# A fp32 encoder block on one core: the second norm's scale by way of HBM, a plain opening of the late up-projection units, and another order of the last steps

## The chip, the cores and the metric

The kernel runs on one core of one Trainium2 chip. A core has five engines with queues of their own, each working its queue strictly in the order in which it was written: TensorE (PE, matrix products, whose weight loads the profile shows as PEld), VectorE (DVE), ScalarE (ACT), GpSimd (POOL) and SyncE (SP). Transfers between HBM and the on-chip memory are issued from SP, ACT or POOL and run on 16 DMA engines. The metric is the device time of one execution in microseconds (us); the kernel before took 945.14 us, the median of three runs (944.67 to 945.18).

## The reference

One layer on x of 256 tokens by 2048 features, everything in float32:

```python
h = _rmsnorm(x, norm1_g)
proj = h @ w_in                                   # q | k | v | u
a = _rmsnorm(_window_attention(q, k, v, sink), attn_out_g)
f = _rmsnorm(_fourier_mix(u, w_fourier), fourier_out_g)
x = x + jnp.concatenate([a, f], axis=-1) @ w_out
x = x + _conv_ffn(_rmsnorm(x, norm2_g), w_up, dw_w, dw_b, w_down)
return _rmsnorm(x, normf_g)

def _conv_ffn(h, w_up, dw_w, dw_b, w_down):
    up = h @ w_up
    gate, val = up[..., :D_FF], up[..., D_FF:]     # D_FF = 5504 = 43 * 128
    gate = conv over the tokens, width 3, per channel (gate, dw_w) + dw_b
    act = jax.nn.gelu(gate, approximate=False) * val
    return act @ w_down
```

The change touches the second norm (its 1/sqrt of the mean square, one number for each token) and the feed-forward part.

## The kernel before, in words

**Two parts for each number.** A float32 product is made of three products of a faster type: each operand is split into a high part (ACT copies it, L180) and a low part (DVE subtracts, L181), and TensorE adds high by high, low by high and high by low into one PSUM bank. A *unit* is one 128x2048 block of weights (1 MB): SP loads it into one of three `raw` buffers (`load`, L160), `split` (L173) makes its parts in one of three `hi` and one of three `lo` buffers and issues the load of the unit three further on, and TensorE then works on it.

**Up-projection units.** For the 43 tiles of 128 channels there are a gate unit and a value unit each. Here the weights stand still and the tokens move (`still_weights`, L322): 16 products of a high weight tile with the high and low parts of the tokens (512 columns) and 16 of a low weight tile with their high parts (256 columns). The order is by default high, low, high, low. With `first = (1, 0)` one high product is taken ahead: high, high, low, high, ..., high, low, low.

**The second norm.** `hT2` holds the tokens turned so that features lie on partitions, scaled by the norm's weight. The other factor, 1/sqrt of the mean square of each token (`rstd_of(tot2, ...)`, a small DVE sum, a DVE multiply and a power on POOL, L279), is multiplied in behind the up-projection: `scaled_sum` (L843) adds the two halves of a unit's bank and multiplies by `r2b`, which has the 256 factors along its columns, the same on all 128 partitions. `spread` (L288) makes `r2b`: DVE builds two diagonal matrices, TensorE multiplies a matrix of ones with them (fp32, L296), DVE copies the bank to `r2b` (L299). The first norm does the same by way of HBM, on POOL's queue (`row_by_hbm`, L303): one transfer writes the 256 numbers as a row, a second reads that row into all partitions.

**Where that stands.** The last unit of the output projection still needs its sums when the feed-forward part begins, so the first two up units, gate0 and val0, are taken as a pair (L1137): twelve of sixteen steps of gate0, then the turning of the last quarter of the tokens (`turn_x(3)`), twelve steps of val0, the last four of both, and then `spread`.

**The feed-forward order.** `ff_items` (L84) writes out one list of items, which TensorE works through: up units ("u"), products of the down-projection ("s": 14 for each of five groups of channel tiles, in a two-level Strassen form with seven products P1, P7, N5, N3, P6, P2, N4 for each of two column halves c, 12 matmuls of 512 columns each, L1070 to L1072) and, in the last group, four "d" items (`("down", c)`, 24 matmuls) for the channel tiles 36 to 39. At the end four `last` units do the tiles 40 to 42 (L1214). `PATTERNS` (L72) gives the order within a group. N5, P6 and N4 use a sum of weight blocks in `sumw`, which POOL's adding transfers build in place: N5's split starts one (L966), P6's the next (L968).

**What an item does to the other queues.** `ff_step(n)` (L992) is called behind item n on TensorE. It first puts the posts of earlier items (`beside`), then the split of item n + 2, then further posts (`behind`). An up unit's posts are `scaled_sum` one item later, then the convolution (`gate_conv`), GELU and, for a value unit, `val_mult` and `act_parts`. A product's bank is added to the output by `product_out` one item later; P1 and N5 stay in their banks and are added by `shared_out` in three steps, the first behind the item that follows P6 of half 1. `down` items 0 and 1 add into the banks of P2 and N4 of the same half (`joined`), items 2 and 3 into banks of their own; `down_out` adds them to the output.

The changed line of the pattern stands for this order from item 141 on, where a number behind a name is the tile and (c=1) the column half:

| item | before | after |
|---|---|---|
| 143 to 149 | N4(c=0), down 0, val 40, P1, N5, gate 41, P7 | the same |
| 150 to 154 | val 41, N3, gate 42, P6, val 42 | N3, val 41, P6, gate 42, val 42 |
| 155 to 159 | P2, down 2, N4, down 1, down 3 | P2, N4, down 1, down 2, down 3 |

In the kernel before, all up units behind the first `down` (val 40, gate 41, val 41, gate 42, val 42) open with `first = (1, 0)`.

Of the kernel before, what the change touches and what calls it, by code (L numbers as in the profile page):

```python
# [8 lines left out]
F32 = mybir.dt.float32  # L9
F32R = mybir.dt.float32r  # L10
AF = mybir.ActivationFunctionType
ALU = mybir.AluOpType

P = 128
D = 2048
S = 256
NK = D // P
# [52 lines left out]


PATTERNS = ["uuu" + "su" * 13 + "s"] * (len(GROUPS) - 1)  # L72
PATTERNS += ["uuu" + "su" * 6 + "sdussu" + "su" * 3 + "sdsdd"]


def group_of(j):
# [7 lines left out]
def ff_items():  # L84


    def ups(first, end):
        return [(kind, j) for j in range(first, end) for kind in ("gate", "val")]

    firsts = [first for first, _ in GROUPS] + [LATE[0], NF]  # L90
    items = ups(0, firsts[1])
    for g, pattern in enumerate(PATTERNS):
        todo = {
            "u": ups(firsts[g + 1], firsts[g + 2]),
            "s": [("product", g, c, p) for c in range(2) for p in PRODUCTS[c]],
            "d": [("down", c) for c in (0, 2, 1, 3)],
        }
        items += [todo[c].pop(0) for c in pattern]
        assert not (todo["u"] or todo["s"]), (g, todo)
    return items + [("last", c) for c in range(4)]  # L100
# [3 lines left out]
def block_kernel(  # L104
# [19 lines left out]
    nc = tc.nc  # L124
    SL = slopes()
    ctx.enter_context(tc.manual_schedule())
    base = ctx.enter_context(tc.tile_pool(name="base", bufs=1))
    wp = ctx.enter_context(tc.tile_pool(name="wp", bufs=1))
    mm = ctx.enter_context(tc.tile_pool(name="mm", bufs=4, space=bass.MemoryType.PSUM))
    dn = ctx.enter_context(tc.tile_pool(name="dn", bufs=4, space=bass.MemoryType.PSUM))  # L130
# [4 lines left out]
    def bank(pool, name):  # L135
        return pool.tile([P, 512], F32, tag=pool.name, name=name)
# [6 lines left out]
    items, up_index = ff_items(), {}  # L143
# [14 lines left out]
    raws, halves = {}, {}  # L158
# [93 lines left out]
    ones = base.tile([P, P], F32, tag="ones", name="ones")  # L252
# [3 lines left out]
    ident = base.tile([P, P], F32, tag="ident", name="ident")  # L256
    make_identity(nc, ident)

    ps = bank(dn, "ps_warm")
# [3 lines left out]
    def vcol(o, n=1):  # L263
        return vec[:, o : o + n]

    def split_scaled(dst, src, g):

        nc.scalar.activation(dst[:, 0:S], src, AF.Copy, scale=g)
        nc.vector.scalar_tensor_tensor(
            dst[:, S : 2 * S], src, g, f32(dst[:, 0:S]), ALU.mult, ALU.subtract  # L270
        )

    def rstd_of(ssq, width, name, n=2, r=None):

        var = base.tile([P, n], F32, tag="var" + name, name="var" + name)
        nc.vector.tensor_scalar(var, ssq, 1.0 / width, EPS, ALU.mult, ALU.add)
        if r is None:
            r = base.tile([P, n], F32, tag="rstd" + name, name="rstd" + name)
        nc.gpsimd.tensor_tensor(r, var, half_pow[:, 0:n], ALU.pow)  # L279
        return r  # L280
# [4 lines left out]
            junk, t[:, b, :], AF.Square, accum_out=parts[:, b, c : c + 1]  # L285
        )

    def spread(r, dst, name):  # L288

        t = wp.tile([P, 512], F32, tag="junk", name=f"diag{name}")  # L290
        dgs = [t[:, b * P : (b + 1) * P] for b in range(2)]
        for b, dg in enumerate(dgs):
            nc.vector.tensor_scalar(dg, ident, r[:, b : b + 1], None, ALU.mult)
        ps = bank(dn, "ps_spread" + name)
        for b in range(2):
            nc.tensor.matmul(  # L296
                ps[:, b * P : (b + 1) * P], ones, dgs[b], start=True, stop=True
            )
        nc.vector.tensor_copy(dst, ps[:, :S])  # L299

    rows = ctx.enter_context(tc.tile_pool(name="rows", bufs=1, space=bass.MemoryType.DRAM))

    def row_by_hbm(r, dst, name):  # L303

        row = rows.tile([2, P], F32, tag="row" + name, name="row" + name)
        nc.gpsimd.dma_start(row.rearrange("b p -> p b"), r)
        nc.gpsimd.dma_start(dst, row.rearrange("b p -> (b p)").partition_broadcast(P))


    def moving_weights(hi, lo, n, kk, act, b, ps, first, last, q0=0):  # L310
# [11 lines left out]
    def still_weights(hi, lo, ps, kk, first=(0, 0)):  # L322

        todo = [list(kk), list(kk)]
        order = [(i, todo[i].pop(0)) for i in range(2) for _ in range(first[i])]
        while todo[0] or todo[1]:
            order += [(i, todo[i].pop(0)) for i in range(2) if todo[i]]  # L330
        for n, (i, k) in enumerate(order):
            x = slice(0, S if i else 2 * S)
            nc.tensor.matmul(  # L333
                ps[:, x], (hi, lo)[i][:, k * P : (k + 1) * P], hk(k)[:, x],
                start=n == 0 and k == 0, stop=n == len(order) - 1 and k == NK - 1,
            )
# [36 lines left out]
    for c in range(4):  # L373
        t = base.tile([P, 4, 512], F32R, tag=f"hT{c}", name=f"hT{c}")
        hT.append(t)
    ps_u = [bank(mm, f"ps_u{b}") for b in range(2)]
    for k in range(NK):
        c, q = k // 4, k % 4
        if q == 0:
            hi, lo = (t.rearrange("p (k c) -> p k c", k=4) for t in parts_of(c))  # L380
        n = 1 if c < 2 else 2
# [390 lines left out]
        yield  # L772
        out_sums(c)

    def turn_x(c):
        turn_x_out(c, turn_x_in(c))

    def turn_x_in(c):
        pss = []
        for q2 in range(2):  # L780
            ps = bank(dn, f"ps_x{c}{q2}")
            for q in range(2):
                for b in range(2):
                    k4 = 2 * q2 + q
                    nc.tensor.transpose(
                        ps[:, q * S + b * P : q * S + (b + 1) * P],
                        xs[c][:, b, k4 * P : (k4 + 1) * P],
                        ident,
                    )
            pss.append(ps)  # L790
        return pss

    def turn_x_out(c, pss):
        t = base.tile([P, 4, 512], F32R, tag=f"hT{c}", name=f"hU{c}")
        for k4 in range(4):
            ps = pss[k4 // 2][:, k4 % 2 * S : (k4 % 2 + 1) * S]
            split_scaled(t[:, k4, :], ps, vcol(V_G2 + 4 * c + k4))
        hT2.append(t)

    at(before, N_OUT + 6, total, sq_a, "a")  # L800
# [2 lines left out]
    for n, (c, kq) in enumerate(OUT_ORDER):  # L803
# [15 lines left out]
        if kq >= 2:  # L819
            part = "a" if kq == 2 else "f"  # L820
            ps = ps_a[c] if kq < 3 else ps_a[c, "f"]
# [311 lines left out]


    pair, joined = [], {}
    first_late = [it[0] for it in items].index("down")
    for q in range(2):  # L1137
        kind, j = items[q]
        ps = bank(mm, f"ps_{kind}{j}")
        pair.append((ps, *halves.pop(n_front + q)))  # L1140
        still_weights(*pair[q][1:], ps, range(12))
        if q == 0:
            ff_step(0)
            turn_x(3)
            hT[:] = hT2
    for ps, hi, lo in pair:
        still_weights(hi, lo, ps, range(12, NK))
    tot2 = base.tile([P, 2], F32, tag="tot2", name="tot2")
    nc.vector.tensor_reduce(tot2, ssq2, mybir.AxisListType.X, ALU.add)
    spread(rstd_of(tot2, D, "2"), r2b, "2")  # L1150
    ff_step(1)
    up_posts(1, *items[0], pair[0][0])
    up_posts(2, *items[1], pair[1][0])
# [1 line left out]
    for n, it in enumerate(items):  # L1155
        if n < 2:
            continue
        if it[0] == "last":
            break
        if n in (2, 3):  # L1160
            ring_load()
        if n == 5:
            pending.append(lambda: first_sums(0, 0))
        if it[0] in ("gate", "val"):
            kind, j = it
            ps = bank(mm, f"ps_{kind}{j}")
            first = (1, 0) if n > first_late else (0, 0)
            still_weights(*halves.pop(up_index[n]), ps, range(NK), first)
            ff_step(n)
            up_posts(n, kind, j, ps)  # L1170
            continue
        if it[0] == "product":
            kind, g, c, p = it
            end = g == len(GROUPS) - 1
            if (c, p) in held:
                by_parts(held[c, p], parts[p], *halves.pop(it), GROUPS[g][1], g == 0, end)
            elif end and p in ("P2", "N4"):
                ps = joined[c, p] = bank(mm, f"ps_{p}{g}{c}")
                by_parts(ps, parts[p], *halves.pop(it), GROUPS[g][1], True, False)
            else:  # L1180
                ps = bank(mm, f"ps_{p}{g}{c}")
                by_parts(ps, parts[p], *halves.pop(it), GROUPS[g][1], True, True)
                at(beside, n + 1, product_out, g, c, p, ps)
            if end and p == ("N4", "P6")[c]:
                for q in range(3):
                    at(behind, n + 1 + (1 + c) * q, shared_out, c, q)
        else:
            kind, c = it
            hi, lo = halves.pop(up_index[n])
            if c < 2:  # L1190
                ps = [joined.pop((c, p)) for p in ("P2", "N4")]
            else:
                ps = [bank(mm, f"ps_l{c}{b}") for b in range(2)]
            for b in range(2):
                moving_weights(hi, lo, 512, LATE, act.get, b, ps[b], c >= 2, True)
            at(beside, n + 1, down_out, c, ps)
            if c == 1:
                gfb = fp.tile([P, D], F32, tag="sumw", name="gfb", bufs=1)
                nc.gpsimd.dma_start(gfb, normf_g.partition_broadcast(P))
        ff_step(n)  # L1200
# [154 lines left out]
```

## Time and profile before

| | |
|---|---|
| median of 3 runs | 945.14 us |
| the profiled execution | 944.62 us |
| its span, first to last instruction | 942.9 us |
| mean granted TensorE clock | 0.999 |
| TensorE busy | 933.8 us, 99% of the span |
| DVE busy | 759.6 us, 81% |
| ACT busy | 541.3 us, 57% |
| POOL busy | 50.6 us, 5% |

The profiled execution is 0.52 us shorter than the median. The page gives busy times over the whole span. The *chain of waits* follows the end of the program back, step by step, to what released each step; each row is a start (us), a length (us), an engine, a tile and a line. The *timeline* of one engine has a start, a length, the instruction and in brackets how long the engine sat idle before it and who released it. The *groups by shape* give, for a stretch, the count, the busy time and the mean duration in ns of equal instructions. The *windows* give, for each stretch, its length and the busy time of each engine, then the granted clock, the busy share of the DMA engines and GB/s. The *DMA issues* give size and time to landing.

### The profile page before, as it was taken

The numbers are of one execution on the slowest core, as the hardware profiler recorded it, in microseconds if no ns is written. First come the engines' busy times: TensorE is split into PE (matmuls) and PEld (weight loads), VectorE is DVE, ScalarE is ACT, GpSimd is POOL, SyncE is SP. The second block draws the span as 40 slices with busy tenths as digits, with TensorE's granted clock in tenths as the row PEclk, the third lists the DMA queues.
The fourth block names the chain that finished last, engine by engine and source line by source line (L and its number), as shares of the span: only waits on it lengthen the run. The fifth ranks groups of instructions, "written<-read, shape, count | busy, mean of one in ns | idle before, by whom it ended". The sixth has DMA issues, their size and how long they took to land.

```text
span 942.9 us, 12805 instructions
## 1 busy us (share of the span) xinstructions
PE 933.8 (99%) x5069; PEld 809.6 (86%) x5069; DVE 759.6 (81%) x948; ACT 541.3 (57%) x659; POOL 50.6 (5%) x67
## 2 busy tenths in 40 slices
PE   9999999999999999999999999999999999999996
PEld 7889998888888888888888888888888888888885
DVE  7668877666677878799887997878988779989896
ACT  7756766454454564566555565555655556655642
POOL 0100000000000000000000000000000000000002
PEclk9999999999999999999999999999999999999999
DMA  9964444446556578877797769787787978779652
GB/s 367 307 224 146 167 146 167 142 171 223 179 220 207 185 235 246 267 253 235 250 273 253 242 231 283 243 265 226 261 245 239 301 242 265 224 237 277 203 179 90
DMA packets 33629, 214.86 MB, mean 228 GB/s; under 512 B 3713, under 2 KB 4225, under 8 KB 10017
## 3 DMA queue, kind: packets, MB, share of 16 engines
q1 hardware_dynamic: 29024, 184.55, 53.0%
q0 software_dynamic: 4544, 29.49, 16.8%
q8 instruction: 40, 0.66, 0.3%
q14 instruction: 21, 0.16, 0.0%
HBM read 211.93 MB, written 2.10 MB: 227 GB/s over the span
## 4 chain that ended last, share of the span: by engine, by line
PE 99%; DMA 0%; DVE 0%; issue 0%; DVEq 0%; POOLq 0%; ACT 0%; POOL 0%
PE ps_val L333 25%; PE ps_gate L333 25%; PE ps_q L333 7%; PE ps_P L1071 3%; PE ps_P L1070 3%; PE ps_P L1072 3%; PE ps_N L1071 3%; PE ps_N L1070 3%; PE ps_N L1072 3%; PE ps_a L318 2%; PE ps_a L316 2%; PE ps_k L333 2%; PE ps_a L317 2%; PE ps_s L637 1%; PE ps_o L709 1%; PE ps_ff L316 1%
## 5 line engine op out<-in xcount | busy, mean ns | idle before, releaser
L181 DVE TENSOR_TENSOR lo<-raw,hi 128x2048 fp32r<-128x2048 f32 (+1 forms) x129 | 293.4, 2275 | 41.0 <-ACT hi L180 40.7
L180 ACT ACTIVATE hi<-raw 128x2048 fp32r<-128x2048 f32 (+1 forms) x129 | 245.5, 1903 | 40.9 <-PE ps_a L317 13.5
L333 PE MATMUL ps_gate<-hU,hi 128*128 128x512 f32 x688 | 236.0, 389 | 0.0
L333 PE MATMUL ps_val<-hU,hi 128*128 128x512 f32 x688 | 235.9, 389 | 0.0
L333 PE MATMUL ps_gate<-hU,lo 128*128 128x256 f32 x688 | 189.6, 276 | 0.0
L333 PE MATMUL ps_val<-hU,lo 128*128 128x256 f32 x688 | 189.4, 276 | 0.0
L333 PEld LDWEIGHTS ps_gate<-hU,hi 128*128 128x128 f32 x688 | 129.1, 188 | 26.8
L333 PEld LDWEIGHTS ps_val<-hU,hi 128*128 128x128 f32 x688 | 129.1, 188 | 26.8
L333 PEld LDWEIGHTS ps_val<-hU,lo 128*128 128x128 f32 x688 | 129.1, 188 | 1.5
L333 PEld LDWEIGHTS ps_gate<-hU,lo 128*128 128x128 f32 x688 | 129.1, 188 | 1.4
L845 ACT ACTIVATE ft_g<-ps_gate 128x256 f32<-128x256 f32 x43 | 16.5, 384 | 123.2 <-PE ps_gate L333 123.2
L845 ACT ACTIVATE ft_v<-ps_val 128x256 f32<-128x256 f32 x43 | 16.5, 384 | 90.8 <-PE ps_val L333 90.8
L333 PE MATMUL ps_q<-hT,hi 128*128 128x512 f32 x192 | 65.2, 392 | 0.0
L1071 PE MATMUL ps_P<-hi_P,op_P 128*128 128x512 f32 x144 | 56.2, 390 | 0.0
L1070 PE MATMUL ps_P<-hi_P,op_P 128*128 128x512 f32 x144 | 56.1, 390 | 0.0
L1072 PE MATMUL ps_P<-lo_P,op_P 128*128 128x512 f32 x144 | 56.0, 389 | 0.0
L333 PE MATMUL ps_q<-hT,lo 128*128 128x256 f32 x192 | 51.1, 277 | 0.0
L962 DVE TENSOR_TENSOR lo_N<-sumw,hi_N 128x2048 fp32r<-128x2048 f32 (+1 forms) x20 | 41.5, 2076 | 9.4 <-ACT hi_N L961 9.2
L1071 PE MATMUL ps_N<-hi_N,op_N 128*128 128x512 f32 x108 | 42.1, 390 | 0.0
L1070 PE MATMUL ps_N<-hi_N,op_N 128*128 128x512 f32 x108 | 42.1, 389 | 0.0
L1072 PE MATMUL ps_N<-lo_N,op_N 128*128 128x512 f32 x108 | 42.0, 389 | 0.0
L333 PEld LDWEIGHTS ps_q<-hT,hi 128*128 128x128 f32 x192 | 35.2, 188 | 6.7
(380 smaller groups left out, 1583.7 us busy)
## 6 DMA issues: line engine op xcount, KB each, us to landing
raw<-in_w_up SPq DMA_DIRECT2D x86, 1024.0 KB, 5.6
raw<-in_w_in SPq DMA_DIRECT2D x20, 1024.0 KB, 4.9
raw<-in_w_out SPq DMA_DIRECT2D x16, 1024.0 KB, 4.8
sumw<-in_w_down POOLq DMA_DIRECT2D x16, 1024.0 KB, 8.7
raw<-in_w_down_late SPq DMA_DIRECT2D x4, 1024.0 KB, 5.9
raw<-in_w_down_last SPq DMA_DIRECT2D x4, 768.0 KB, 4.3
ux<-in_w_u_x SPq DMA_DIRECT2D x3, 768.0 KB, 9.2
xs<-in_x SPq DMA_DIRECT2D x4, 512.0 KB, 16.5
```

What stands on the lines that cost most here:

```text
L180: nc.scalar.activation(hi[:, 0:n], raw[:, 0:n], AF.Copy)
L181: nc.vector.tensor_tensor(lo[:, 0:n], raw[:, 0:n], f32(hi[:, 0:n]), ALU.subtract)
L316: nc.tensor.matmul(ps, ah, wh, start=first and q == q0, stop=False)
L317: nc.tensor.matmul(ps, al, wh, start=False, stop=False)
L318: nc.tensor.matmul(ps, ah, wl, start=False, stop=last and q == q0 + len(kk) - 1)
L333: nc.tensor.matmul(ps[:, x], (hi, lo)[i][:, k * P : (k + 1) * P], hk(k)[:, x], start=n == 0 and k == 0, stop=n == len(order) - 1 and k == ...
L637: nc.tensor.matmul(ps[:, b * S : (b + 1) * S], qT[:, qo + b * P : qo + (b + 1) * P], kT[:, ko : ko + S], start=n == 0, stop=n == 2,)
L845: nc.scalar.activation(tmp, ps[:, S : 2 * S], AF.Copy)
L962: nc.vector.tensor_tensor(lo, src, f32(hi), ALU.subtract)
L1070: nc.tensor.matmul(ps, o[:, 0, p, :], hi[:, s], start=first and p == 0, stop=False)
L1071: nc.tensor.matmul(ps, o[:, 1, p, :], hi[:, s], start=False, stop=False)
L1072: nc.tensor.matmul(ps, o[:, 0, p, :], lo[:, s], start=False, stop=last and p == n - 1)
```

## The change

1. `spread` is gone. The sum `tot2` and its 1/sqrt are written ahead of the turning of the last quarter's parts. Behind the first of that turning's four steps ACT issues the transfer of the 256 factors to HBM (`row_out`), and behind the fourth the transfer of that row into `r2b` on all partitions (`row_in`), which waits for the first to land. The first norm's row goes as before.
2. No up unit has `first = (1, 0)` any more: the five late ones open high, low like the others.
3. The last pattern is written differently (table above), and the `down` items are loaded and run in the order 0, 1, 2, 3. The three `down` items behind N4 now follow it directly, and gate 42 and val 42 follow each other.

```diff
-PATTERNS += ["uuu" + "su" * 6 + "sdussu" + "su" * 3 + "sdsdd"]
+PATTERNS += ["uuu" + "su" * 6 + "sdu" + "ssu" * 2 + "suuss" + "ddd"]
...
-            "d": [("down", c) for c in (0, 2, 1, 3)],
+            "d": [("down", c) for c in range(4)],
...
-    def spread(r, dst, name):
-
-        t = wp.tile([P, 512], F32, tag="junk", name=f"diag{name}")
-        dgs = [t[:, b * P : (b + 1) * P] for b in range(2)]
-        for b, dg in enumerate(dgs):
-            nc.vector.tensor_scalar(dg, ident, r[:, b : b + 1], None, ALU.mult)
-        ps = bank(dn, "ps_spread" + name)
-        for b in range(2):
-            nc.tensor.matmul(
-                ps[:, b * P : (b + 1) * P], ones, dgs[b], start=True, stop=True
-            )
-        nc.vector.tensor_copy(dst, ps[:, :S])
-
+    def row_out(engine, r, name):
+
+        row = rows.tile([2, P], F32, tag="row" + name, name="row" + name)
+        engine.dma_start(row.rearrange("b p -> p b"), r)
+        return row
+
+    def row_in(engine, row, dst):
+
+        engine.dma_start(dst, row.rearrange("b p -> (b p)").partition_broadcast(P))
+
     def row_by_hbm(r, dst, name):
-
-        row = rows.tile([2, P], F32, tag="row" + name, name="row" + name)
-        nc.gpsimd.dma_start(row.rearrange("b p -> p b"), r)
-        nc.gpsimd.dma_start(dst, row.rearrange("b p -> (b p)").partition_broadcast(P))
+        row_in(nc.gpsimd, row_out(nc.gpsimd, r, name), dst)
...
-    def turn_x_out(c, pss):
+    def turn_x_out(c, pss, behind_first=None):
         t = base.tile([P, 4, 512], F32R, tag=f"hT{c}", name=f"hU{c}")
         for k4 in range(4):
             ps = pss[k4 // 2][:, k4 % 2 * S : (k4 % 2 + 1) * S]
             split_scaled(t[:, k4, :], ps, vcol(V_G2 + 4 * c + k4))
+            if k4 == 0 and behind_first:
+                behind_first()
         hT2.append(t)
...
         if q == 0:
             ff_step(0)
-            turn_x(3)
+            pss = turn_x_in(3)
+            tot2 = base.tile([P, 2], F32, tag="tot2", name="tot2")
+            nc.vector.tensor_reduce(tot2, ssq2, mybir.AxisListType.X, ALU.add)
+            r2, row2 = rstd_of(tot2, D, "2"), []
+            turn_x_out(3, pss, lambda: row2.append(row_out(nc.scalar, r2, "2")))
+            row_in(nc.scalar, row2[0], r2b)
             hT[:] = hT2
     for ps, hi, lo in pair:
         still_weights(hi, lo, ps, range(12, NK))
-    tot2 = base.tile([P, 2], F32, tag="tot2", name="tot2")
-    nc.vector.tensor_reduce(tot2, ssq2, mybir.AxisListType.X, ALU.add)
-    spread(rstd_of(tot2, D, "2"), r2b, "2")
     ff_step(1)
...
-            first = (1, 0) if n > first_late else (0, 0)
-            still_weights(*halves.pop(up_index[n]), ps, range(NK), first)
+            still_weights(*halves.pop(up_index[n]), ps, range(NK))
```

More of the change, by code (lines that the diff above doesn't have):

```diff
@@ L773, in out_post @@
         out_sums(c)
-    def turn_x(c):
-        turn_x_out(c, turn_x_in(c))
     def turn_x_in(c):
@@ L1135, in block_kernel @@
     pair, joined = [], {}
-    first_late = [it[0] for it in items].index("down")
     for q in range(2):
```

## Prediction

> **What bounds the kernel now.** I read the page first, then the chain of waits, then, for the two places that the change touches (near 260 us and behind 850 us), the timelines of ACT, DVE and SP, the groups by shape and the windows.
>
> ```profile
> PE 933.8 (99%) x5069; PEld 809.6 (86%) x5069; DVE 759.6 (81%) x948; ACT 541.3 (57%) x659; POOL 50.6 (5%) x67
> ```
>
> TensorE is busy 933.8 of 942.9 us. The chain of waits, start and length in us, is TensorE in nearly every row, at both places:
>
> ```profile
> 264.81 1.36 PE ps_gate L333 x8
> ...
> 267.54 0.44 PE ps_spread L296 x4
> 267.98 5.45 PE ps_gate L333 x32
> ...
> 833.75 5.44 PE ps_val L333 x32
> 841.91 5.44 PE ps_gate L333 x32
> ...
> 866.56 5.45 PE ps_gate L333 x32
> ...
> 874.79 5.45 PE ps_val L333 x32
> 883.03 5.45 PE ps_gate L333 x32
> 891.26 5.45 PE ps_val L333 x32
> 934.07 0.44 DVE xs L1085
> ```
>
> So the kernel ends when TensorE's queue ends, plus the tail from 934.07 on. What is taken off TensorE's queue is gained in full, as long as no other queue is then late. Two things are to be seen. The spread costs 0.44 us on the chain with no gap about it. And an up unit plus a product took 841.91 - 833.75 = 8.16 us ahead of the first "down" item, but 883.03 - 874.79 = 8.24 and 891.26 - 883.03 = 8.23 behind it. The groups by shape, first for the stretch 800 to 849.9 us and below the dots for 860.85 to 900 us, say where:
>
> ```profile
> L1071 PE MATMUL ps_P<-hi_P,op_P 128*128 128x512 f32 x14 | 5.4, 389 | 0.0
> L1070 PE MATMUL ps_P<-hi_P,op_P 128*128 128x512 f32 x13 | 5.1, 389 | 0.0
> ...
> L1071 PE MATMUL ps_P<-hi_P,op_P 128*128 128x512 f32 x16 | 6.4, 398 | 0.0
> L1070 PE MATMUL ps_P<-hi_P,op_P 128*128 128x512 f32 x16 | 6.3, 394 | 0.0
> ```
>
> The same product instruction is 5 to 9 ns longer in the late stretch; no engine is waited for in either.
>
> **Part 1, the scale by HBM: what it removes.** TensorE loses the four fp32 passes of the spread: 0.44 us, the chain's row above. DVE loses two diagonals and one copy; they lie beside TensorE's work and I count them as nothing.
>
> **Part 1: what it adds.** Two transfers on ACT's queue, a wait of ACT for POOL's power ahead of the first, and a wait for the first transfer's landing ahead of the second. The timelines, ACT's rows first, then DVE's, and one issue on SP's queue:
>
> ```profile
> 262.75 0.47 ACT L268 ACTIVATE hU<-ps_x,vec 128x256 fp32r<-128x256 f32 x1 [0.58 <-DVE hU L269]
> 266.10 1.91 ACT L180 ACTIVATE hi<-raw 128x2048 fp32r<-128x2048 f32 x1 [2.87 <-PE ps_gate L333]
> ...
> 257.49 2.29 DVE L181 TENSOR_TENSOR lo<-raw,hi 128x2048 fp32r<-128x2048 f32 x1 [0.97 <-ACT hi L180]
> ...
> 263.66 0.15 DVE L1149 TENSOR_REDUCE tot<-ssq 128x2 f32<-128x8 f32 x1
> 264.82 0.48 DVE L293 TENSOR_SCALAR diag<-ident,rstd 128x128 f32<-128x128 f32 x2 [0.80 <-POOL rstd L279]
> 271.01 0.42 DVE L848 TENSOR_TENSOR fa_g<-fa_g,r2b 128x256 f32<-128x256 f32 x1
> ...
> 855.05 0.33 SPq L945 DMA_DIRECT2D rawd41d<-in_w_down  x1
> ```
>
> The sum, the multiply and POOL's power took from 263.66 to 264.82, 1.16 us. Moved ahead of the hU steps they begin when DVE ends its low part, at 257.49 + 2.29 = 259.78, so the factors are ready at 260.9. The first transfer then stands between ACT's first and second hU step. An issue by SP occupies its queue for 0.33 us (the last row), so it is done at 261.3. DVE's and ACT's hU steps alternate, and the last began at 262.75; TensorE wants their result from 264.81 on. DVE's step behind the last ends by 263.7, so there is a slack of about 1 us: nothing lost.
>
> The second transfer blocks ACT until the row has landed, and behind it stands the split of val1 (the row at 266.10, held there by its buffer, which TensorE releases). So a landing within 5.2 us of 260.9 costs nothing at all. TensorE begins gate1 at 267.54 without the spread, and wants val1's low part at 267.54 + 5.44 + 0.23 = 273.2 (0.23 is the high product's share of the 5.44 / 16 = 0.34 us of a pair); ACT's 1.91 and DVE's 2.29 us ahead of it allow the split to start as late as 269.0, so 8.1 us cost TensorE nothing. DVE multiplies by `r2b` at 271.01, and its next low part is wanted 5.44 us after val1's, so `r2b` may land some 4 us later still before TensorE notices.
>
> No row shows a transfer on ACT's queue. The nearest rows are two: the output's stores on SP's queue, and the first norm's two transfers on POOL's queue:
>
> ```profile
> out_y<-xs SPq DMA_DIRECT2D x2, 128.0 KB, 1.9
> r1b<-row POOLq DMA_DIRECT2D x1, 128.0 KB, 7.0
> row<-rstd POOLq DMA_DIRECT2D x1, 1.0 KB, 10.5
> ```
>
> Bounds for both together: 2 x 1.9 = 3.8 us and 10.5 + 7.0 = 17.5 us, so `r2b` is there between 264.7 and 278.4. The first norm's transfers ran among loads; these do so only at first:
>
> ```profile
> 261.00:264.00 3.00, 3.00 (x20) 2.64 (x19) 1.88 (x6) 1.31 (x3) 0.00 (x0) 1.00 0.84 330
> 264.00:267.00 3.00, 3.00 (x20) 2.65 (x19) 0.50 (x3) 0.90 (x1) 0.69 (x1) 1.00 0.00 0
> 267.00:270.00 3.00, 3.00 (x21) 2.72 (x20) 1.98 (x2) 3.00 (x3) 0.00 (x0) 1.00 0.00 0
> ```
>
> The DMA share is 0.84 until 264 and 0.00 from there to 270. I take the first transfer as landed at 264 to 265 and the second at 266.5 to 268, near the stores: hidden, with 3 us to spare. Part 1 gives -0.44 us.
>
> [...]
>
> **Part 2, the plain opening.** The number of matmuls stays. The late units end on two low products, and what follows them runs slower. TensorE's timeline at the start of val 40 and at the first `last` product, with one row of DVE's for gate 41:
>
> ```profile
> 855.38 0.63 PE L333 MATMUL ps_val<-hU,hi 128*128 128x512 f32 x2
> ...
> 918.51 0.39 PE L1221 MATMUL ps_e<-hi,act 128*128 128x512 f32 x1
> ...
> 863.27 2.29 DVE L181 TENSOR_TENSOR lo<-raw,hi 128x2048 fp32r<-128x2048 f32 x1 [0.45 <-ACT hi L180]
> ```
>
> Between the first two it needs 63.13 us for five up units, seven products and three down items. At the earlier rates (5.44 for a unit, 8.16 - 5.44 = 2.72 for 12 matmuls of 512 columns, so 5.44 for 24) they are worth 5 x 5.44 + 7 x 2.72 + 3 x 5.44 = 62.56 us. The difference, 0.57 us, goes if the opening is its cause: the slow stretch begins right behind the first such unit, and no wait is shown. The bounds are 0 (another cause) and 0.57 us; I take 0.57. What the early high product covered is a low part that comes up to 0.23 us late. The closest is gate 41's, done at 863.27 + 2.29 = 865.56, against a unit that begins at 866.56 on the chain, so nothing is late next from this alone.
>
> **Part 3, the order.** TensorE's work is the same, DVE's and ACT's too, POOL and SP issue the same transfers. What moves is who is late. In the new order TensorE at the clean rates ends val 42 at 855.38 + 5 x 5.44 + 5 x 2.72 = 896.2, P2 at 898.9, N4 at 901.6, down 1, 2 and 3 at 907.1, 912.5 and 917.9, where the first `last` product begins (918.51 now). The rows for what follows, a window first, then DVE's, ACT's and SP's timelines, and a kind of transfer:
>
> ```profile
> 898.00:912.00 14.00, 14.00 (x63) 11.45 (x62) 13.93 (x16) 6.69 (x5) 0.56 (x1) 1.00 0.59 209
> ...
> 901.78 2.28 DVE L181 TENSOR_TENSOR lo<-raw,hi 128x2048 fp32r<-128x2048 f32 x1
> ...
> 907.33 3.95 DVE L181 TENSOR_TENSOR lo<-raw,hi 128x2048 fp32r<-128x2048 f32 x2
> 919.44 1.28 DVE L1077 TENSOR_TENSOR xs<-ps_l,xs 128x512 f32<-128x512 f32 x2
> 920.64 1.75 DVE L181 TENSOR_TENSOR lo<-raw,hi 128x1536 fp32r<-128x1536 f32 x1
> ...
> 896.75 0.39 ACT L845 ACTIVATE ft_v<-ps_val 128x256 f32<-128x256 f32 x1 [2.30 <-PE ps_val L333]
> 916.24 1.49 ACT L1211 ACTIVATE hi<-raw 128x1536 fp32r<-128x1536 f32 x1 [1.70 <-DMA raw<-in_w_down_last]
> ...
> 904.09 7.54 SPq L164 DMA_DIRECT2D raw<-in_w_down_last  x3
> ...
> sumw<-in_w_down POOLq DMA_DIRECT2D x2, 1024.0 KB, 8.3
> ```
>
> DVE is the engine to watch, since the stretch 898 to 912 is full already now (13.93 of 14.00 us). Behind val 42 (896.2) ACT reads its bank (0.39), makes down 1's high part and is done at 898.6. From there DVE has no gap (each instruction counted 0.08 shorter than its row, as the next begins that early): low part of down 1, 2.2, done 900.8; three adds 1.85; val 42's product 0.34; low part of down 2, done 905.2; activations' low part 0.34; low part of down 3, done 907.7; four adds 2.4; the first `last` unit's low part (1536 columns) 1.75, done 911.85. These low parts are wanted at 902.1, 907.5 and 913.0 (two matmuls, 0.45, behind each start), so all three down items are in time. But the load of the fourth `last` unit waits for that last instruction. Now it is issued at 911.3 (904.09 + 7.54 less 0.33) and ACT takes it at 916.24, 4.95 us later; then it comes at 916.8. The code splits this fourth unit ahead of the third: ACT 1.49, DVE 1.75, two adds 1.2, and only then the third unit's low part, 1.75, done at 923.05. TensorE wants it at 917.94 + 2 x 2.04 + 0.45 = 922.5 (a `last` product has 9 matmuls, 2.72 x 9 / 12 = 2.04). I take a stall of 0.6 us. Its bounds: 0, if the load lands 0.6 us sooner, and 3.9, if that load took the 8.3 us of the adding transfers.
>
> **The sum.** 944.62 - 0.44 - 0.57 + 0.58 = 944.2 us for an execution like the profiled one. The median of the runs shown is 0.52 above it, so I say 944.7 us. Parts 2 and 3 nearly cancel: if the opening isn't the cause of the slow products, TensorE comes 0.5 us later to the `last` units and the stall shrinks to about 0.1, which gives the same time. With neither stall nor slow products it is 944.1.
>
> **The rivals.** (a) *The row is late, slower.* If the first transfer takes the 10.5 us of the first norm's row, ACT is free at 271.4, val1's low part comes at 275.6 instead of 273.2, and TensorE stalls 2.4 us; with 7.0 for the second, `r2b` is there at 278.4, the following low part at 281.1, about when TensorE, itself late, wants it. 944.7 + 2.4 = 947.1. It decides from a landing of 8.1 us on, and passes 0.2% over the time before (1.9 us) only near the full 10.5. For it: the only row of such a transfer; against it: idle DMA engines from 264 on. [...] Chance 0.11. (b) *The load of the fourth `last` unit is slow, slower.* A stall of 3.9 instead of 0.6: 948.0. Against it: the DMA share is under 0.6 in that stretch. Chance 0.05. (c) *The spread hid something, or the order frees more than I see, faster.* All known gains together are 1.0 us; to pass 0.2% another 0.9 us must turn up, say if the tail from 934.07 to the end, 9 us, shortened. Nothing shows that it would: 942.9. Chance 0.06. (d) *Part 1 is hidden but the stall is larger or absent*: 944.1 to 946.0, part of the forecast.
>
> **How the numbers follow.** 0.2% of 945.14 is 1.9 us, about what a measurement of this kernel tells from no change. The forecast (944.1 to 946.0) has 0.78; (a) 0.11, (b) 0.05, (c) 0.06. Faster by over 0.2%: 0.06; within: 0.78; slower: 0.16. The range reaches from 943.4, the clean case on a run somewhat shorter than the shortest shown (944.67 - 1.0 = 943.7), to 946.6, part of the way to (a), and leaves out (a)'s full price, (b) and (c).
>
> **What would show it.** Part 1: no ps_spread row, ACT's r2b transfer landing before 270, the first gate's multiply no later than 271, and gate1 starting 0.4 us sooner. Part 2: product matmuls of 389 ns behind val 40. Part 3: an idle TensorE ahead of the third `last` product, released by DVE's low part. Wrong it would be if ACT's split of val1 began after 269.0, if TensorE waited for any down item's low part, or if the products stayed at 398 ns.

## The result, and the profile after

The changed kernel took 947.97 us (median of 10 runs, 945.63 to 963.41), the kernel before on the same chip 945.11 us (10 runs, 944.63 to 945.99): 1.0024 times as long, with a 95% interval of 1.0015 to 1.0033. That is 2.9 us or 0.3% slower by the medians, outside the range of 943.4 to 946.6. The ratio leaves out the two runs over 960 us, as disturbed ones; the experiments show that they belong to the change. Together with three repeats the 13 times lie in three levels: 945.6 and 945.8; eight from 947.3 to 948.2; three from 961.6 to 963.4. The profile that came with the result is that of the 945.63 us run, so it shows only the lowest level.

Section 1 of its page, in which TensorE is as full as before:

```profile
span 943.8 us, 12798 instructions
PE 933.3 (99%) x5065; PEld 808.9 (86%) x5065; DVE 758.6 (80%) x945; ACT 541.0 (57%) x659; POOL 50.6 (5%) x67
```

Its chain of waits (start, length, what):

```profile
260.56 9.28 DMA row<-rstd
...
269.91 0.33 ACTq L298
...
270.35 1.93 ACT hi L180
...
272.30 2.30 DVE lo L181
...
274.64 5.53 PE ps_val L327 x31
```

and its table of TensorE's waits:

```profile
PE ps_val L327 <- DVE lo L181: 1.7, 1, 1.7
```

Before, the chain ran through TensorE here. Now the last 14 us ahead of val 1's low part run outside TensorE: the row's way to HBM, ACT's second transfer, the split of val 1 on ACT and DVE, and only then TensorE again. The spread's row of 0.44 us is gone, and a gap of 1.7 us stands in its place.

Where the row's 9.28 us go is seen in the kinds of transfer, the DMA queues for 262 to 264.2 us, and the windows (the last two columns are the DMA share and GB/s):

```profile
r2b<-row ACTq DMA_DIRECT2D x1, 128.0 KB, 4.6
row<-rstd ACTq DMA_DIRECT2D x1, 1.0 KB, 9.3
```
```profile
q10 hardware_dynamic: 272, 0.00, 7.0%
```
```profile
262.00:264.00 2.00, 2.00 (x14) 1.76 (x13) 1.16 (x3) 0.61 (x2) 0.00 (x0) 1.00 0.91 357
264.00:270.00 6.00, 6.00 (x37) 5.33 (x36) 0.00 (x0) 0.00 (x0) 0.00 (x0) 1.00 0.00 0
```

All 272 packets of the row (its 256 pieces of 4 bytes and 16 more) are over by 264.2, and the engines then stand still. The landing is reported at 269.84. So some 5.7 of the 9.3 us pass behind the last packet with no traffic at all.

In the late stage the groups by shape (861 to 900 us) show the products back at 389 ns (one group stands for all), and TensorE's timeline the starts of val 40, of the first `last` unit, and the one late matmul in the third:

```profile
L1063 PE MATMUL ps_P<-hi_P,op_P 128*128 128x512 f32 x16 | 6.2, 389 | 0.0
```
```profile
856.67 0.39 PE L327 MATMUL ps_val<-hU,hi 128*128 128x512 f32 x1
...
919.28 0.39 PE L1214 MATMUL ps_e<-hi,act 128*128 128x512 f32 x1
...
923.93 0.50 PE L1216 MATMUL ps_e<-lo,act 128*128 128x512 f32 x1
```

From val 40 to the first `last` unit it is 919.28 - 856.67 = 62.61 us, 0.52 less than the 63.13 of before. Behind that, 0.2 us are lost about 923.9.

The balance of this execution against the profiled one before: start of val 40 later by 856.67 - 855.38 = 1.29 us (a gap of 1.73 less the spread's 0.44), then 0.52 gained and 0.2 lost: about 1.0, against the spans' 943.8 - 942.9 = 0.9. That is the lowest level. The other 2 us of the median it does not show.

### The profile page after: what moved, and what is told of

Same layout as the page of the kernel before. It is cut to its first block, busy times and chain, and to the rows that moved or that the text cites. A ratio compares the mean times of both kernels' runs of the same rounds, so it can differ in the third digit from the quotient of the medians.

```text
span 943.8 us, 12798 instructions
## 1 busy us (share of the span) xinstructions
PE 933.3 (99%) x5065; PEld 808.9 (86%) x5065; DVE 758.6 (80%) x945; ACT 541.0 (57%) x659; POOL 50.6 (5%) x67
## 4 chain that ended last, share of the span: by engine, by line
PE 90%; issue 7%; DMA 1%; DVE 1%; ACT 0%; POOL 0%; DVEq 0%; POOLq 0%; ACTq 0%
PE ps_val L327 24%; PE ps_gate L327 24%; PE ps_q L327 7%; PE ps_P L1063 3%; PE ps_P L1064 3%; PE ps_P L1065 3%; PE ps_N L1063 3%; PE ps_N L1064 3%; PE ps_N L1065 3%; PE ps_k L327 2%; DMA row<-rstd 1%; PE ps_a L312 1%; PE ps_a L311 1%; PE ps_a L310 1%; PE ps_s L631 1%
```

## The experiments

Four ideas stood at the start. T1: ACT, held by its second transfer until the row lands, is what makes the gap, and the row's landing differs from run to run and so makes the levels. T2: the row is late because of the loads. T3: the levels belong to the new order or opening. T4: the slow landing was a single case. T5 to T7 came on the way.

**The HBM scale alone.**

```
-PATTERNS += ["uuu" + "su" * 6 + "sdu" + "ssu" * 2 + "suuss" + "ddd"]
+PATTERNS += ["uuu" + "su" * 6 + "sdussu" + "su" * 3 + "sdsdd"]
-            "d": [("down", c) for c in range(4)],
+            "d": [("down", c) for c in (0, 2, 1, 3)],
...
+            first = (1, 0) if n > first_late else (0, 0)
```

> The kernel before with part 1 alone: the scale goes by HBM on ACT's queue, the opening and the late order are those of before. Theory T1 (the row lands late and ACT, whose next instruction is the second transfer, is held until then; its landing differs from run to run): the same gap of TensorE ahead of val 1 as in the changed kernel, 1.7 us at a landing of 9.3 us, so 945.11 - 0.44 + 1.73 = 946.4 us in the runs like the profiled one, and runs 2 to 2.5 us above those, as in the changed kernel. Rival T3 (the gap of 1.7 us is all that part 1 does, and the runs near 948 come from the late order or the opening): one level near 946.4, and no run near 948.5. Rival T4 (the slow landing belongs to the profiled execution alone): one level at 944.7.

Measured: 946.63 us (before 944.78), nine runs: 946.0 to 947.2 six times, 948.65, 948.9 and 961.49. The profile (946.17 us) has a landing of 9.2 us and a gap of 1.7 us. T3 and T4 fall: the loss and its levels come with part 1.

**The order and the opening alone.** The reverse: spread as before, the four lines on the order in the diff above the other way round, and no `first`.

> The kernel before with parts 2 and 3 alone: plain opening of all units and the new late order, the spread by TensorE stays. T1: one narrow level at 945.11 - 0.69 (products of 389 instead of 394 to 398 ns, as the changed kernel's stretch from val 40 to the first last unit showed) + 0.10 (a late low part of the third last unit) = 944.5 us, and no gap ahead of val 1. T3: two or three levels up to 3 us apart here as well, so a median at or over 946.

Measured: 944.80 us, eleven runs from 944.12 to 945.09, one level; 1.0000 of before, interval 0.9991 to 1.0008. The profile has no gap at val 1, 62.61 us from val 40 to the first `last` unit, and 0.34 us lost at the third. Net 63.13 - 62.61 - 0.34 = 0.2 us, too little for the medians to show.

**The second transfer behind the split of val 1.**

```
-            row_in(nc.scalar, row2[0], r2b)
     ff_step(1)
+    row_in(nc.scalar, row2[0], r2b)
```

> The changed kernel with the second transfer issued behind ACT's split of val 1, so that ACT is not held by the row while that split is wanted. T1: no gap ahead of val 1. With a landing of 9.3 us r2b comes at about 275, DVE's next low part at 277.6, before TensorE wants it at about 278.4: 945.11 - 0.44 - 0.59 = 944.1 us. With a landing of 11.5 us r2b comes near 277 and the low part behind the multiply near 279.9: a gap of 1.5 us there, 945.6 us. So lower than the changed kernel by 1.7 to 2.3 us in either level. If something else than ACT's being held makes the gap (T5, the transfers themselves slow TensorE or the loads): as the changed kernel, 945.7 to 948.

Measured: 944.88 us, eleven runs: nine from 944.14 to 945.6, then 947.94 and 959.38. In the profile the landing is 9.0 us, and there is no gap: ACT's being held was the cause of it, and T5 falls. But DVE now waits for `r2b`:

```profile
276.92 0.42 DVE L841 TENSOR_TENSOR fa_g<-fa_g,r2b 128x256 f32<-128x256 f32 x1 [4.67 <-DMA r2b<-row]
277.26 2.28 DVE L181 TENSOR_TENSOR lo<-raw,hi 128x2048 fp32r<-128x2048 f32 x1
```

The low part behind it is done at 277.26 + 2.28 = 279.54. In TensorE's timeline gate 2 begins at 279.31, so it wants this low part at 279.31 + 0.23 = 279.54, and its second matmul is the one in this row:

```profile
279.60 0.39 PE L327 MATMUL ps_gate<-hU,lo 128*128 128x256 f32 x1
```

So nothing is left, and a run in which the row is a little later would have a gap again, at the next unit. That fits the two runs over 947 us, of which there is no profile. The median is 0.8 us over the 944.1 expected; why stays open.

**Writes of other shapes, read by nobody.** The scale goes by TensorE's spread, the row is still written, and eight more writes follow:

```
+        8: lambda: probe("rowB", nc.scalar, [2, P], r2, "b p -> p b"),
+        11: lambda: probe("rowC", nc.scalar, [P, 2], r2),
+        14: lambda: probe("rowD", nc.scalar, [P, P], r2b[:, 0:P]),
...
+        20: lambda: probe("rowF", nc.gpsimd, [2, P], r2, "b p -> p b"),
+        23: lambda: probe("rowG", nc.sync, [2, P], r2, "b p -> p b"),
...
```

rowB, rowF, rowG and rowI are 256 pieces of 4 bytes, rowC and rowH 128 of 8 bytes, rowD 128 of 512 bytes, rowE one of 1 KB.

> The changed kernel with the scale by TensorE's spread again, the row still written at the same place but read by nobody, and further such writes in the up units behind it: the same 256 pieces of 4 bytes on ACT's, POOL's and SP's queues (rowB, rowI, rowF, rowG), 128 pieces of 8 bytes (rowC, rowH), 128 pieces of 512 bytes (rowD), one piece of 1 KB (rowE). T1 in the form that the confirmation of many small writes takes long: rowA, rowB, rowI near 9 us whatever the loads do, rowC and rowH shorter, about half, rowD and rowE near the stores' 1.9 us. T2 (the row is slow because loads are under way when it is issued): rowB to rowI long for every shape wherever the DMA share is high, and short where it is low. The time is the same by all: 945.11 - 0.59 = 944.5 us, a little more if the issues (0.4 us of ACT each) delay a split.

The kinds of transfer:

```profile
rowD<-r2b ACTq DMA_DIRECT2D x1, 64.0 KB, 4.3
...
row<-rstd ACTq DMA_DIRECT2D x1, 1.0 KB, 9.5
rowB<-rstd ACTq DMA_DIRECT2D x1, 1.0 KB, 11.8
rowC<-rstd ACTq DMA_DIRECT2D x1, 1.0 KB, 5.1
...
rowF<-rstd POOLq DMA_DIRECT2D x1, 1.0 KB, 11.4
rowG<-rstd SPq DMA_DIRECT2D x1, 1.0 KB, 11.1
rowH<-rstd ACTq DMA_DIRECT2D x1, 1.0 KB, 14.7
rowI<-rstd ACTq DMA_DIRECT2D x1, 1.0 KB, 11.6
```

The row's shape takes 9.5 to 11.8 us on any of three queues, while 64 times its bytes (rowD) take 4.3. The 8-byte pieces are inconclusive (5.1 and 14.7). With no reader the time is 944.68 us, eight runs in one level: the write itself costs nothing. The one-piece write has no landing in the trace. T2 falls for the larger part of the 9 us: here too the row's packets are over by 265 us, and it lands at 261.04 + 9.5 = 270.5. Loads may have a share in the 3 us ahead of its packets, and among loads the same shape takes 11.1 to 11.8.

**Pieces of 8 bytes for the row itself.**

```
+        row = rows.tile([P, 2], F32, tag="row" + name, name="row" + name)
+        engine.dma_start(row, r)
...
-        nc.vector.tensor_tensor(add, add, r2b, ALU.mult)
+        y = add.rearrange("q (b p) -> q b p", b=2)
+        nc.vector.tensor_tensor(y, y, r2b.rearrange("q (p b) -> q b p", b=2), ALU.mult)
```

> The changed kernel with the row written as 128 pieces of 8 bytes instead of 256 of 4; the second transfer reads it as it lies, and DVE's multiply takes the factors in that order. Theory T1a (what is late is the confirmation behind the last packet of 256 pieces of 4 bytes, 5.7 us in the changed kernel and 7.3 us for rowB of the probes, against 1.3 us for rowC's 128 pieces of 8 bytes): the row lands in 5 to 5.5 us, under the 7.6 us from which TensorE waits, so no gap ahead of val 1, one level of runs, and 0.44 + 0.15 us less than before (0.15 is what the new order and opening gave in their own run's stretches): 944.2 us where before is 944.8. Rival T1b (any small write by ACT may be confirmed late, as rowH's 14.7 us): gaps and levels as in the changed kernel, 946 to 948.

Measured: 944.13 us where before is 944.96 us; 0.9991 of it, interval 0.9982 to 1.0; eleven runs from 943.67 to 945.32, one level. The kinds of transfer, and ACT's timeline:

```profile
row<-rstd ACTq DMA_DIRECT2D x1, 1.0 KB, 5.2
```
```profile
261.10 0.34 ACTq L303 DMA_DIRECT2D row<-rstd  x1
...
266.36 0.33 ACTq L308 DMA_DIRECT2D r2b<-row  x1
266.79 1.92 ACT L180 ACTIVATE hi<-raw 128x2048 fp32r<-128x2048 f32 x1 [3.11 <-PE ps_gate L337]
```

The split waits for its buffer again, not for a transfer, and no wait at val 1 is left: T1a's 5 to 5.5 us came (the packets are over by 265 us as before, and the landing at 266.3 now follows in under 2 us), and T1b falls. This is the fastest of the versions, 3.8 us below the changed kernel by the medians; against the one before its 0.8 us are not clear of the noise, since the interval reaches 1.0.

**The opening alone and the order alone.** In the first, before without `first`; in the second, before with the changed patterns and the `first` rule kept.

> The kernel before with the plain opening alone (part 2), late order and spread as before. If the opening makes the slow products: 62.6 us instead of 63.1 from val 40 to the first last product, products of 389 ns behind val 40, 0.5 us less in all unless a low part comes late. Rival (the order makes them): 63.1 us and products of 394 and 398 ns.

> The kernel before with the new late order alone (part 3), the opening with an early high product kept. If the opening makes the slow products: 63.1 us from val 40 to the first last product, products of 394 and 398 ns, and TensorE comes 0.5 us later to the third last unit, so the gap there is near 0. Rival (the order makes them): 62.6 us and products of 389 ns, with a gap of 0.2 to 0.4 us at the third last unit.

Measured: 944.35 and 944.87 us (before 944.96; the intervals of both hold 1). From val 40 to the first `last` unit 62.70 us with the opening alone, 63.10 with the order alone. The groups by shape of the order alone (861 to 900 us):

```profile
L1071 PE MATMUL ps_P<-hi_P,op_P 128*128 128x512 f32 x16 | 6.4, 398 | 0.0
L1070 PE MATMUL ps_P<-hi_P,op_P 128*128 128x512 f32 x16 | 6.3, 394 | 0.0
```

So the opening made the slow products, in either order. At the third `last` unit's low part TensorE lost 0.17 us with the opening alone and 0.08 with the order alone (0.34 with both): so the plain opening, with which TensorE is there sooner, has a share in that loss, in the old order too.

**Many small writes.** As the earlier probes, but every fifth item writes on ACT's queue, in the turns A B A C A D:

```
+        if kind == "A":
+            t = rows.tile([2, P], F32, tag=f"pA{n}", name=f"pA{n}")
+            nc.scalar.dma_start(t.rearrange("b p -> p b"), r2)
+        elif kind == "B":
+            t = rows.tile([P, 2, 128], F32, tag=f"pB{n}", name=f"pB{n}")
+            nc.scalar.dma_start(t[:, :, 0], r2)
+        elif kind == "C":
+            t = rows.tile([P, 2], F32, tag=f"pC{n}", name=f"pC{n}")
+            nc.scalar.dma_start(t, r2)
...
+            t = rows.tile([P, 1], F32, tag=f"pD{n}", name=f"pD{n}")
+            nc.scalar.dma_start(t, r2[:, 0:1])
```

> The changed kernel with the scale by TensorE's spread and 28 small writes on ACT's queue through the up units, read by nobody: A, 256 pieces of 4 bytes as the row (14 times); B, 256 pieces of 4 bytes in pairs 512 bytes apart; C, 128 pieces of 8 bytes side by side; D, 128 pieces of 4 bytes side by side. T1a by the number of 4-byte pieces: 5 to 8 us behind the last packet for A and B, half for D, 1 to 1.5 us for C. By their closeness in HBM: B short, D half of A. And if the levels of the changed kernel come from the row's landing, A's landings spread by 2 us and more over the 14, with perhaps one near 25 us. The rival that the wait is for the loads: the time behind the last packet follows the DMA share, not the shape. The time of the kernel: 944.7, within 0.3.

The kinds of transfer (the median of each):

```profile
pA<-rstd ACTq DMA_DIRECT2D x14, 1.0 KB, 11.5
pB<-rstd ACTq DMA_DIRECT2D x5, 1.0 KB, 3.3
pC<-rstd ACTq DMA_DIRECT2D x5, 1.0 KB, 7.1
pD<-rstd ACTq DMA_DIRECT2D x4, 0.5 KB, 16.4
```

One by one: A 8.0 to 19.3 us, B 2.0 to 4.3, C 2.9 to 8.5, D 15.9 to 17.4. The number of pieces is not it: B has as many as A, D half of them. What goes with the time is how close the pieces lie in HBM: 4 bytes apart (A, D) was slow, 512 bytes apart (B) quick. Neither account had D right: both made it half of A. The time was wrong too: 973.5 us (two runs, 971.74 and 975.26) instead of 944.7. The windows show how (DMA share and GB/s at the end), and the chain the load that was late for it:

```profile
780.00:820.00 40.00, 37.77 (x209) 32.32 (x208) 31.27 (x34) 19.57 (x20) 1.72 (x2) 1.00 0.90 187
```
```profile
852.91 15.15 DMA sumw<-in_w_down
```

At a share of 0.90 the engines move 187 GB/s, where in the same window of the changed kernel they move 234 at 0.77. The loads that shared the engines with these writes were held up: those of the up weights took 10.3 us to landing in the median of 86, in the changed kernel 5.7. TensorE's waits add up to 16 of the 27 us between the spans of this run and of the earlier probes (970.0 and 943.0); the rest stays open.

**The changed kernel again, three times, for the levels.**

> The changed kernel once more, for the profile of an execution near 948 us (six of its ten earlier runs). T1: the other stretches are as in the profiled one (587.6 us from gate 1 to val 40 less the gap, 62.6 us from there to the first last product), the row's landing is about 11.5 us instead of 9.3 and the gap ahead of val 1 is 3.9 us instead of 1.7. Rival: the landing is 9.3 us again and the 2.2 us lie elsewhere, in the late stage or in the second transfer.

> As the run before it: in an execution near 948 us the row lands after about 11.5 us and the gap ahead of val 1 is about 3.9 us; in one near 945.7 us 9.3 and 1.7.

> As the run before it: in an execution near 948 us the row lands after about 11.5 us and the gap ahead of val 1 is about 3.9 us; in one near 945.7 us 9.3 and 1.7.

They took 948.07, 961.56 and 947.28 us, and T1's account of the levels falls: the row lands in 9.8, 9.7 and 9.4 us, and the gap is 1.8 us in each. The chain and three windows of the run of 947.28 us (the granted clock is the third column from the end), then the chain of the one of 961.56 us:

```profile
274.95 7.09 PE ps_val L327 x31
```
```profile
272.00:275.00 3.00, 1.17 (x8) 0.77 (x6) 2.40 (x2) 2.64 (x3) 0.00 (x0) 1.00 0.12 44
275.00:278.00 3.00, 3.00 (x10) 2.62 (x11) 2.97 (x4) 2.28 (x4) 0.00 (x0) 0.51 0.70 199
278.00:281.00 3.00, 3.00 (x18) 2.63 (x17) 2.90 (x7) 2.77 (x4) 0.00 (x0) 0.92 1.02 418
```
```profile
275.06 5.63 PE ps_val L327 x31
280.69 5.60 PE ps_gate L327 x32
...
772.26 5.60 PE ps_val L327 x32
```

In the first, TensorE's clock is half right behind the gap, and val 1 takes 7.09 us instead of 5.53. These 1.56 us are nearly the whole distance of 1.7 us between its span of 945.5 us and the 943.8 of the lowest level. By the windows the halved stretch is (0.49 + 0.08) x 3 / 0.5 = 3.4 us long. In the second the clock stays at 1.00, but from the gap on each unit takes 5.60 us instead of 5.44. The groups by shape for 277 to 850 us, of the run of 961.56 us and then of the lowest level:

```profile
L327 PE MATMUL ps_gate<-hU,hi 128*128 128x512 f32 x608 | 214.5, 395 | 0.0
L327 PE MATMUL ps_gate<-hU,lo 128*128 128x256 f32 x608 | 170.6, 281 | 0.0
L1065 PE MATMUL ps_P<-lo_P,op_P 128*128 128x512 f32 x123 | 49.0, 398 | 0.0
```
```profile
L327 PE MATMUL ps_gate<-hU,hi 128*128 128x512 f32 x624 | 214.1, 389 | 0.0
L327 PE MATMUL ps_gate<-hU,lo 128*128 128x256 f32 x624 | 172.2, 276 | 0.0
L1065 PE MATMUL ps_P<-lo_P,op_P 128*128 128x512 f32 x128 | 49.8, 389 | 0.0
```

The matmuls of the up units are 5 to 6 ns longer, and the three kinds of a product's matmuls take 388, 392 and 398 ns (the last is shown) where all took 389, with no wait, until the first "down" item near 869 us. There are 78 units and 63 products in that stretch, and a product has grown from 2.72 to 2.77: 78 x 0.16 + 63 x 0.05 = 15.6 of the 16.0 us between the spans.

**A gap without any transfer.** The order-and-opening kernel with the spread, and copies on ACT ahead of val 1's split, so that its low part comes late; five of them, then three:

```
+    spin = wp.tile([P, 512], F32, tag="junk", name="spin")
+    for _ in range(5):
+        nc.scalar.activation(spin, xs[0][:, 0, :], AF.Copy)
```

> The kernel of the new order and opening with the spread by TensorE (no transfer of the scale), and five copies of 128x512 on ACT, read by nobody, ahead of its split of val 1, so that TensorE has a gap of about 1.7 us ahead of val 1's low part. T6 (what follows the gap comes from the gap): the levels of the changed kernel come back: 944.8 + 1.7 = 946.5 us in some runs, about 948.2 in others (half the granted clock for 3.4 us), and perhaps one in five near 962. Rival T7 (they come from the transfers): one level at 946.5.

> As e10 with three copies: a gap of about 0.65 us. T6 with a length from which the clock is halved that lies between 0.65 and 1.7 us: one level at 944.8 + 0.65 = 945.4 us, without halved clock; runs near 960 only if the slow pace needs no long gap. T7: the same 945.4 and no run above it.

Measured with five copies: 947.81 us, twelve runs: 946.6 to 947.0 six times, 948.65 to 949.04 four times, 964.06 and 965.47. The three levels are back without a transfer, and T7 falls. TensorE's waits and the chain of a run of 949.04 us show the same picture:

```profile
PE ps_val L333 <- DVE lo L181: 1.8, 1, 1.8
```
```profile
276.32 7.14 PE ps_val L333 x31
283.46 5.44 PE ps_gate L333 x32
```

With three copies: 944.95 to 946.48 us four times, 960.85 to 961.32 eight times. The gap of the profiled run, one of 960.85 us, is a third as long, its clock is not halved, and by the times two runs in three have the slow pace. Three of the other four lie within 0.3 us; the one of 946.48 us is 1.2 us above them, and a halved clock in it is not excluded. The waits and the chain of the profiled run:

```profile
PE ps_val L333 <- DVE lo L181: 0.6, 1, 0.6
```
```profile
274.37 5.63 PE ps_val L333 x31
280.00 5.60 PE ps_gate L333 x32
```

Runs near 960 us were expected only if the slow pace needs no long gap. It needs none: here they are the common case.

## Why the prediction was wrong

**The step that failed** is in part 1, on what is added: "I take the first transfer as landed at 264 to 265 ... near the stores: hidden, with 3 us to spare". The row's packets had indeed passed by 264.2, but its landing came at 269.84. The choice between the two nearest rows went by the loads under way (the DMA share 0.84, then 0.00), and those were not what the first norm's 10.5 us were made of. The trace of the kernel before has this already: the 32 packets that it shows of the first norm's row lie between 42 and 44 us, and the landing came at 38.96 + 10.5 = 49.5, over 5 us behind them. The rows alike were the two of the same shape, 256 pieces of 4 bytes: 10.5 on POOL's queue, 9.3 here, 9.0 to 10.1 in the other profiles of it on ACT's. The stores of 1.9 us write 128 KB each and have another shape.

**The limits were nearly right.** A landing of 8.1 us was said to cost TensorE nothing; the gap of 1.73 at 9.28 puts that limit at 7.55. Left out were 0.5 us from the landing to the start of the split (269.84 to 270.35), in which ACT issues the second transfer. The sign named beforehand, the split of val 1 after 269.0, came true with 270.35. The second transfer took 4.6 us, and DVE's multiply came at 274.96, not by 271.

**Rival (a) was the mechanism**, with a gap of 2.4 us at 10.5 us; by the same slope 1.2 at 9.3, and 1.7 with the 0.5 us left out. Its 947.1 us is near the measured 947.97, but not from its own terms alone: 945.11 - 0.44 for the spread - 0.3 for parts 2 and 3 together in the profiled run + 1.8 for the gap is 946.2, the lowest level or a little over it, and the halved clock adds 1.56 to the common one: 947.7. That a gap costs more than its length was in no part of the prediction.

**Part 1's gain** fits: the spread's row is gone from the chain, and with the quick row (the 8-byte pieces) the kernel is 0.8 us below before by the medians, where 0.44 and the 0.3 make 0.7. Its interval reaches 1.0, so the times alone do not show it.

**Part 2** was right: 0.57 us said, 0.52 measured, products of 389 ns, and the opening is the cause, since it makes the difference alone and the order does not.

**Part 3** was right in place and too large in size: 0.6 us said, and 0.2 measured at the third `last` unit's low part; 0.34 in the order-and-opening run. The wait is DVE's, as named. The load of the fourth unit was the term: from its issue at 913.37 to ACT's start on it at 917.73 it took 4.36 us instead of 4.95. The order was not the only cause, since the opening alone shows 0.17 there. That parts 2 and 3 nearly cancel is what their own run shows (944.80 against 944.78). Rivals (b) and (c) did not come: the late load was not slow, and nothing else got faster.

## What to carry to other kernels

Price a transfer by the row that has its shape (pieces, their size and their distance in HBM), not by the row that has its bytes: here 1 KB in pieces of 4 bytes took 9.3 us, and 64 KB in pieces of 512 bytes 4.3. Look up whether the engines were idle while it was pending: here they were for 5.7 of the 9.3 us, so the loads were not what held it that long, and with another layout, in 8-byte pieces, it landed after 5.2. Ahead of an instruction that blocks an in-order engine, ask which instruction of another stage stands behind it there (here the split of val 1, which began at 270.35). And a gap of a TensorE that is otherwise full must be counted with what follows it: put no step where its slack is a few tenths of a microsecond if a miss may cost fifteen microseconds (here a gap of 0.6 us went with times near 961 us in 8 of 12 runs).

## What the runs showed of the hardware that was not expected

- Writes of 4-byte pieces side by side in HBM landed 8 to 19 us after their issue, also 5.7 us after their last packet with the engines idle; as many pieces 512 bytes apart took 2.0 to 4.3 us. What makes the close ones slow no run shows.
- A gap of 1.8 us in a TensorE that was full otherwise was followed by half the granted clock for 3.4 us in some executions (0.51 over 3 us in the run of 947.28 us; with the gap made by ACT, by their times six of twelve had neither this nor the slow pace). With 0.6 us the one profile does not show it; one of the twelve times leaves it open. Why only some executions have it the runs do not show.
- A late low part can also start a slow pace at full clock: 395 instead of 389 ns and 281 instead of 276 ns for hundreds of matmuls, until the first "down" item. By the times it came in 8 of 12 runs with a gap of 0.6 us, in 2 of 12 with 1.8 us, in 3 of 13 of the changed kernel, and in none of the 46 runs of five kernels without a late low part in this stretch (order and opening, the first probes, opening alone, order alone, 8-byte pieces). With the second transfer behind the split, where the next unit's low part had no slack, one run of eleven lies near 960 too. The late products of the kernel before (398, 394 and 387 ns for their three kinds) look like a relative of it, started by its opening. What keeps it going and what ends it stays open.
